# A block's second MLP product: its output gate multiplied into the weights in DRAM, the residual preloaded into accumulators, sums placed at other steps

## The chip, the cores and the metric

The kernel runs on one core of one Trainium2 chip. The metric is the device time of one execution in microseconds (us). TensorE (PE) multiplies matrices into PSUM, VectorE (DVE) and GpSimd (POOL) do elementwise work, ScalarE (ACT) does functions and copies, and SyncE (SP) issues the transfers between DRAM and SBUF, in the order of its queue.

## The reference

One layer of a diffusion block: modulation, three token mixers, an output projection into a gated residual, then a squared-ReLU MLP into a second gated residual, and a final RMS norm. The change touches only the last lines:

```python
x = x + gt1 * (y_lat @ w_out)
x = x + gt2 * (square(relu(modulate(rmsnorm(x, g_mlp), sh2, sc2) @ w_mlp1 + b_mlp1)) @ w_mlp2 + b_mlp2)
return rmsnorm(x, g_final)      # x: 1024 tokens x 1024, w_mlp1: 1024 x 4096, w_mlp2: 4096 x 1024
```

`gt2` (g2 below) is one number for each of the 1024 output columns.

## The kernel before

**Arithmetic.** All large products are done in f32 with two fp32r parts: each operand is split into a high part (a copy by ACT) and a low part (a subtraction by DVE, line 1277), and each product becomes three matmuls. Both MLP products use the seven-product scheme of Winograd for 2 x 2 blocks, so sums and differences of operand blocks are formed first (`qop`, line 1304, on DVE) and sums of results afterwards.

**First product** (`prod1`, `op1`). The 4096 hidden columns are eight f-blocks of 512. Each f-block is seven products, n = 0 to 55 over all; `op1(n + 4)` prepares the operand of a product four ahead and, at an f-block's first product, loads its four quarters of w_mlp1 (line 1301). Each product is 24 matmuls into two PSUM banks. Results go through DVE sums and two ACT passes into one of two staging buffers and from there to DRAM tensor `HD` (line 1365).

**Second product** (`prod2`, `op_ab`, `blk_load`). The 4096 rows of w_mlp2 are taken as f-block 0, then the pairs (1,2), (3,4), (5,6): four blocks `b` of seven products `m` in the order 1, 2, 5, 6, 3, 7, 4. Each product is four PSUM tiles of 128 x 512 (6 matmuls each in block 0, 12 in the others). They are added over the blocks into `PART[1]` to `PART[7]`, four tiles each; in block 0 an ACT copy (line 1563) starts them, in the others DVE adds them (line 1565). `PART[2]` to `PART[5]` are the tiles `acc`, which end as the four quarters of the output. Operands come from a ring `QR` of eleven buffers, among them the two halves of the tile named `rw` and the units `qxh`, `qxl`, `qt`, `uu`.

**Last product.** f-block 7 is multiplied without the scheme: for each of eight token tiles (i, t) and both column halves h, 12 matmuls into one bank, added to the accumulator (line 1623). Its operands are split by `last_op`; those named `lop` (keys b11 and b21) lie in a new tile that takes the place of `rw`. Before this addition the seven sums are folded into the four accumulators (`fold`, line 1524, DVE), each accumulator is multiplied by g2 (line 1536, POOL, 16 instructions), and x2, the first residual with g2 x b_mlp2 already in it, is added from buffers that `x2_load` fills (line 1537, DVE, 16 instructions); two of these buffers are halves of `rw` and a unit `qxl`. Since the accumulators are scaled before f-block 7 comes in, that f-block's weights are multiplied by g2 when they are loaded (line 1460, POOL, 4 loads). Then follow squares for the norm (ACT), the reciprocal root (POOL, line 1629), the scaling (DVE, line 1633) and the store.

**Order.** The program is written in one order; a scheduler ahead of time gives each engine's queue its order from priorities (the written order) and its own estimate of when each instruction is ready. On the chip each queue runs strictly in its order.

Of the kernel before, what the change touches and what calls it, by code (L numbers as in the profile page):

```python
# [7 lines left out]
F32 = mybir.dt.float32  # L8
F32R = mybir.dt.float32r
AF = mybir.ActivationFunctionType  # L10
ALU = mybir.AluOpType
# [4 lines left out]
P = 128  # L16
D = 1024
# [21 lines left out]
def body(nc, tc, a, out):  # L39
    V, S, G, T, SY = nc.vector, nc.scalar, nc.gpsimd, nc.tensor, nc.sync  # L40
# [100 lines left out]
    drp = est.enter_context(pool("drp", space=DRAM))  # L141
# [310 lines left out]
    for d in range(2):  # L452
        r = slice(64 + 32 * d, 96 + 32 * d)
# [275 lines left out]
    with ExitStack() as st:  # L729
# [10 lines left out]
        for hb in range(2):  # L740
            SY.dma_start(out=WRG[64 * hb:64 * hb + 64, :, 64 * hb:64 * hb + 64],
                         in_=a["w_rg"][0].rearrange("d g (t hb) c e -> hb c (d g t) e", hb=2)[hb])
# [425 lines left out]
    X2D = drp.tile([8, P, D], F32, name="X2D")  # L1168
# [4 lines left out]
    g2B = p2a.tile([P, D], F32, name="g2B")  # L1173
    AX1 = p2a.tile([P, 2048], F32, name="ax1")
    AX2 = p2a.tile([P, 1536], F32, name="ax2")
# [88 lines left out]
    w1, w2 = a["w_mlp1"][0], a["w_mlp2"][0]  # L1264
# [5 lines left out]
    def half(ap, n):  # L1270
        return ap.rearrange("p (a n) -> p a n", n=n)
# [34 lines left out]
    def op1(n):  # L1306
        fb, m = n // 7, n % 7
        if fb >= 8:
            return
        q = ORDER1[m]  # L1310
        src = rq[AIN[q]]
        if n < 2:
            src = WRAW
            w1_load(0, AIN[q], src)
        if m == 0:
            for k in ("21", "22", "11", "12"):
                w1_load(fb, k, rq[k])
        if q == 6:
            e = G if n < 7 else V
            qop(rq, "21", "21", "22", ALU.add, e)  # L1320
            qop(rq, "11", "21", "11", ALU.subtract, e)
        elif q == 7:
            qop(rq, "21", "22", "11")
        elif q == 3:
            qop(rq, "12", "12", "11")
        d = R1[(0, 1, 0, 1, 2, 3, 4)[n] if n < 7 else (n - 7) % 6]
        split(src, d[:, 0:1024], d[:, 1024:2048])
        ops1.append(tuple(half(d[:, i:i + 1024], 256) for i in (0, 1024)))
# [95 lines left out]
    prod1(4)  # L1424
    op1(7)
    op1(8)
    for n in range(5, 56):
        prod1(n)
        op1(n + 4)


    ORDER = (1, 2, 5, 6, 3, 7, 4)
# [12 lines left out]
    def cacc(i, h, t):  # L1445
        return PART[2 + 2 * i + h][t]

    def q_load(n, key, fbs, dst):
        r, c = int(key[1]) - 1, int(key[2]) - 1
        if key[0] == "a":  # L1450
            src = HD[fbs[c], r] if len(fbs) == 2 else HD[fbs[0], r, :, 2 * c:2 * c + 2, :]
        else:
            r0, nr = (fbs[r] * 512, 512) if len(fbs) == 2 else (fbs[0] * 512 + r * 256, 256)
            src = w2[r0:r0 + nr, 512 * c:512 * c + 512].rearrange("(s p) c -> p s c", p=P)
        d = half(dst, 512)
        ld[0] = SY.dma_start(out=d, in_=src)
        if key[0] == "b" and fbs == (7,):
            for s_ in range(0, d.shape[1], 2):
                o = d[:, s_:s_ + 2, :]
                G.tensor_tensor(out=o, in0=o, in1=g2B[:, 512 * c:512 * c + 512].unsqueeze(1).broadcast_to([P, 2, 512]), op=ALU.mult)  # L1460

    QS = {}

    def blk_load(b, keys):
        q = QS.setdefault(b, {})
        for k in keys:
            if b == 0:
                u = LOADS.index(k)
                d = XAu[u // 2][:, 1024 * (u % 2):1024 * (u % 2) + 1024]
            else:  # L1470
                d = QR[qn[0] % len(QR)]
                qn[0] += 1
            q[k] = d
            q_load(b, k, BLK[b], d)
# [36 lines left out]
    def blk_t1(b):  # L1511
        if b < len(BLK):
            qop(QS[b], "b12", "b12", "b11")
# [8 lines left out]
    def fold(o, x0, x1, ts=range(4)):  # L1522
        for t in ts:
            V.tensor_tensor(out=PART[o][t], in0=PART[x0][t], in1=PART[x1][t], op=ALU.add)  # L1524

    X2U = {}

    def x2_load():
        for (i, h), k in zip(((0, 0), (0, 1), (1, 1), (1, 0)), ("b11", "b21", "a22", "b12")):
            X2U[i, h] = u = half(QS[NBK - 1][k], 512)  # L1530
            SY.dma_start(out=u, in_=X2D[4 * i:4 * i + 4, :, 512 * h:512 * h + 512].rearrange("t p c -> p t c"))

    def residual(i, h, ts=range(4)):
        for t in ts:
            o = cacc(i, h, t)
            G.tensor_tensor(out=o, in0=o, in1=g2B[:, 512 * h:512 * h + 512], op=ALU.mult)  # L1536
            V.tensor_tensor(out=o, in0=o, in1=X2U[i, h][:, t, :], op=ALU.add)

    LQ, LO = {}, {}

# [14 lines left out]
    def prod2(b, m):  # L1555
        q = ORDER[m]
        oa, ob = OA.pop(0), OB.pop(0)
        for t in range(4):
            ps = pP.get([P, 512])
            mm3(ps, oa, ob, slice(t * P, t * P + P), True, True)  # L1560
            o = PART[q][t]
            if b == 0:
                S.activation(out=o, in_=ps, func=AF.Copy)
            else:
                V.tensor_tensor(out=o, in0=o, in1=ps, op=ALU.add)  # L1565

    blk_load(0, LOADS)
    blk_t1(0)
    op_ab(0, 0)
    op_ab(0, 1)  # L1570
# [2 lines left out]
    for b in range(NBK):  # L1573
        fin = b == NBK - 1
        for m in range(7):
            if m == 0 and not fin:
                with tc.issue_after(ld[0].ins):
                    blk_load(b + 1, LOADS[:3])
            if m == 0 and fin:
                last_load((0, 2, 4))  # L1580
            prod2(b, m)
            if m < 5:
                op_ab(b, m + 2)
            if m == 4 and not fin:
                blk_load(b + 1, LOADS[3:])
                blk_t1(b + 1)
            if m >= 5:
                op_ab(b + 1, m - 5)
            if fin and m == 4:
                last_load((6,))  # L1590
                ow = units(ml.tile([P, 4096], F32R, tag="rw", name="lop"))
                last_op("b11", ow[0])
                last_op("b21", ow[1])
            if fin and m == 5:
                for k, u in zip(("a11", "a12", "b12", "b22"), RAu[e5:e5 + 2] + RBu[e5:e5 + 2]):
                    last_op(k, u)
                rF = QS[b]["a12"][:, 0:1024]
                bcast_row(rF, a["g_final"])
                x2_load()
                fold(7, 7, 6)  # L1600
                fold(5, 5, 7)
                residual(0, 0)
            if fin and m == 6:
                last_op("a21", RAu[2 - e5])
                last_op("a22", RAu[3 - e5])
                residual(0, 1)
            if fin and m == 3:
                fold(6, 6, 1)
                fold(2, 2, 1)
                fold(1, 6, 5)  # L1610
            if fin and m == 4:
                fold(3, 3, 1)
    pP = Sub(PD[0][:2] + pp)
    for i in range(2):
        for t in range(4):
            tc_ = slice(t * P, t * P + P)
            ss = p2a.tile([P, 6], F32, tag="ss3", bufs=4, name="ss3")
            for h in range(2):
                ps = pP.get([P, 512])
                for j in range(2):  # L1620
                    mm3(ps, LO[f"a{i + 1}{j + 1}"], LO[f"b{j + 1}{h + 1}"], tc_, j == 0, j == 1)
                o = cacc(i, h, t)
                V.tensor_tensor(out=o, in0=o, in1=ps, op=ALU.add)
                S.activation(out=psx, in_=o, func=AF.Square, scale=1.0 / 32, accum_out=ss[:, 4 + h:5 + h])
                if i + t == 4:
                    V.tensor_tensor(out=WX[h], in0=o, in1=rF[:, 512 * h:512 * h + 512], op=ALU.mult)
            rs = ss[:, 2:3]
            V.tensor_scalar(out=ss[:, 1:2], in0=ss[:, 4:5], scalar1=ss[:, 5:6], scalar2=EPS, op0=ALU.add, op1=ALU.add)
            G.tensor_tensor(out=rs, in0=ss[:, 1:2], in1=MHALF, op=ALU.pow)
            for h in range(2):  # L1630
                o, dst = cacc(i, h, t), out[0, (4 * i + t) * P:(4 * i + t + 1) * P, 512 * h:512 * h + 512]
                if i + t < 4:
                    V.scalar_tensor_tensor(out=o, in0=o, scalar=rs, in1=rF[:, 512 * h:512 * h + 512], op0=ALU.mult, op1=ALU.mult)
                elif h == 0:
                    S.activation(out=o, in_=WX[h], func=AF.Copy, scale=rs)
                else:
                    V.tensor_scalar(out=o, in0=WX[h], scalar1=rs, scalar2=None, op0=ALU.mult)
                SY.dma_start(out=dst, in_=o)
            if i == 0:
                fold(4, 4, 7, (t,))  # L1640
                residual(1, 0, (t,))
                residual(1, 1, (t,))
    est.close()


# [21 lines left out]
```

## Time and profile before

| | |
|---|---|
| median of three runs | 1337.53 us (1336.25 to 1340.71) |
| the profiled execution, whole | 1332.67 us |
| its span, first to last instruction | 1331.0 us |
| mean granted TensorE clock | 0.979 |
| busy: PE / DVE / ACT / POOL | 93% / 73% / 44% / 20% of the span |
| DMA | 148.64 MB, 33.5% of 16 engines' time |

All rows of the trace have times in us from the span's start. The first product runs in about 703 to 989, the second in 989 to 1259, the last in 1259 to the end. A matmul's end is modelled, so consecutive starts, not durations, give the pace of PE.

### The profile page before, as it was taken

What the parts mean: (1) busy time and instruction counts of PE and PEld (TensorE: products, weight loads), DVE (VectorE), ACT (ScalarE), POOL (GpSimd) and SP (SyncE); (2) the same over time, 40 slices, a digit from 0 to 9 for tenths busy, and PEclk for the clock granted to TensorE, in tenths of its full rate; (3) what the DMA queues carried; (4) which work ended last, traced back from release to release, by engine and by line L of the source; (5) the groups of instructions that cost most, each with busy time, mean ns of one, the idle gap of its engine ahead of it and who ended that gap; (6) DMA issues with size and microseconds to landing.
All of it is one profiled execution on the core that took longest, in us unless ns stands there. A gap on an engine that the chain in (4) does not pass through costs nothing.

```text
span 1331.0 us, 16443 instructions
## 1 busy us (share of the span) xinstructions
PE 1242.2 (93%) x6146; PEld 974.1 (73%) x6146; DVE 972.1 (73%) x1414; ACT 587.7 (44%) x938; POOL 260.3 (20%) x291
## 2 busy tenths in 40 slices
PE   5889998899999899999979999999999999999957
PEld 1567676787786577777857888888888888888746
DVE  4796795888774566775598665555485979899975
ACT  4648653433433434453456444445467333333212
POOL 3321123123220334313650000000000000110541
PEclk9998999999999999999989999999999999999979
DMA  9422233232234221153325322233294050512202
GB/s 326 141 79 84 90 104 95 80 100 92 92 99 119 80 56 56 54 184 136 104 78 174 111 95 95 95 127 127 73 359 153 31 222 1 201 53 80 95 16 111
DMA packets 102483, 148.64 MB, mean 112 GB/s; under 512 B 8870, under 2 KB 62852, under 8 KB 100868
## 3 DMA queue, kind: packets, MB, share of 16 engines
q1 hardware_dynamic: 102404, 147.60, 33.5%
q8 instruction: 48, 0.79, 0.2%
q14 instruction: 31, 0.25, 0.1%
HBM read 116.62 MB, written 30.95 MB: 111 GB/s over the span
## 4 chain that ended last, share of the span: by engine, by line
PE 59%; DVE 10%; POOL 3%; DMA 3%; issue 2%; ACT 2%; POOLq 0%; DVEq 0%; ACTq 0%; SPq 0%
PE pp L53 26%; PE pd L53 19%; PE psx L53 6%; PE psa L53 2%; PE psb L53 2%; POOL acc L1536 1%; PE pst L53 1%; DMA wx<-in_w_out_dram 1%; PE psl L53 1%; PE pst L942 1%; DVE acc L1524 1%; DVE yl L1152 1%; DMA wx<-ZD 1%; DVE rbd L842 1%; DVE yt L1277 1%
## 5 line engine op out<-in xcount | busy, mean ns | idle before, releaser
L53 PE MATMUL pd<-xl,wht 128*128 128x512 f32 (+1 forms) x304 | 124.3, 413 | 5.0 <-DVE xl L235 4.1
L53 PE MATMUL pd<-xh,wlt 128*128 128x512 f32 (+1 forms) x304 | 125.3, 414 | 1.2 <-POOL cp L395 0.7
L53 PE MATMUL pd<-xh,wht 128*128 128x512 f32 (+1 forms) x304 | 124.0, 413 | 1.2 <-ACT cp L647 0.6
L1460 POOL TENSOR_TENSOR qt<-qt,g2B 128x1024 f32<-128x1024 f32 x4 | 11.5, 2902 | 461.1 <-DMA qt<-in_w_mlp_dram 461.1
L352 POOL TENSOR_TENSOR wlt<-wraw,wht 128x512 fp32r<-128x512 f32 x40 | 57.3, 1434 | 177.7 <-ACT wht L351 165.5
L53 PE MATMUL pp<-ya,wlt 128*128 128x512 f32 x188 | 71.8, 391 | 0.0
L53 PEld LDWEIGHTS pd<-xl,wht 128*128 128x128 f32 (+1 forms) x304 | 57.5, 189 | 18.2 <-DVE xl L235 5.7
L53 PE MATMUL pp<-yb,wlt 128*128 128x512 f32 x176 | 68.6, 390 | 0.0
L53 PE MATMUL pp<-ya 128*128 128x512 f32 x176 | 68.5, 389 | 0.0
L53 PEld LDWEIGHTS pd<-xh,wht 128*128 128x128 f32 (+1 forms) x304 | 57.5, 189 | 13.9 <-ACT cp L647 1.0
L53 PEld LDWEIGHTS pd<-xh,wlt 128*128 128x128 f32 (+1 forms) x304 | 57.4, 189 | 14.0 <-issue 1.9
L53 PE MATMUL pd<-ob,yb 128*128 128x512 f32 x220 | 66.8, 396 | 0.0
L727 DVE SCALAR_TENSOR_TENSOR wx<-wx,SCL,wx 128x512 f32<-128x512 f32 x56 | 44.3, 791 | 23.9 <-DMA wx<-in_w_ada_dram 23.6
L351 ACT ACTIVATE wht<-wraw 128x512 fp32r<-128x512 f32 (+2 forms) x50 | 28.6, 580 | 65.8 <-PE pd L53 22.5
L1536 POOL TENSOR_TENSOR acc<-acc,g2B 128x512 f32<-128x512 f32 x16 | 36.8, 2319 | 74.9 <-PE pp L53 52.8
L1304 DVE TENSOR_TENSOR rw<-rw 128x1024 f32<-128x1024 f32 (+1 forms) x31 | 39.9, 1290 | 13.1 <-DMA rw<-in_w_mlp_dram 12.7
L53 PE MATMUL pp<-ob,yb 128*128 128x512 f32 x152 | 46.2, 406 | 2.7 <-DVE acc L1565 2.7
L53 PEld LDWEIGHTS pd<-ob,yb 128*128 128x128 f32 x220 | 41.3, 188 | 9.9
L1276 ACT ACTIVATE ya<-rw 128x1024 fp32r<-128x1024 f32 x26 | 27.4, 1059 | 43.4 <-PE pp L53 22.9
L1362 ACT ACTIVATE pp<-pp,V 128x512 f32<-128x512 f32 x40 | 26.4, 661 | 41.2 <-DVE pp L1357 41.0
L53 PE MATMUL psx<-xc,wht 128*128 128x256 f32 (+1 forms) x192 | 41.7, 297 | 1.2 <-POOL xc L235 0.7
L1357 DVE TENSOR_TENSOR pp<-pp,uu 128x512 f32<-128x512 f32 x40 | 27.8, 696 | 19.6 <-PE pp L53 19.4
(805 smaller groups left out, 3498.6 us busy)
## 6 DMA issues: line engine op xcount, KB each, us to landing
wx<-in_w_ada_dram SPq DMA_DIRECT2D x64, 256.0 KB, 2.8
rw<-in_w_mlp_dram SPq DMA_DIRECT2D x32, 512.0 KB, 4.0
wraw<-in_w_in_dram SPq DMA_DIRECT2D x44, 256.0 KB, 3.1
ada<-in_w_ada_dram SPq DMA_DIRECT2D x16, 512.0 KB, 5.5
HD<-wraw SPq DMA_DIRECT2D x16, 512.0 KB, 3.3
HD<-g1B SPq DMA_DIRECT2D x16, 512.0 KB, 3.0
XB<-XSD SPq DMA_DIRECT2D x19, 256.0 KB, 2.9
xin<-in_x_dram SPq DMA_DIRECT2D x8, 512.0 KB, 5.5
```

Of the source, the lines that this page charges most:

```text
L53: return T.matmul(o, l, r, start=start, stop=stop)
L351: S.activation(out=ph, in_=pr, func=AF.Copy)
L352: (V if split or name[0:2] == "xr" else G).tensor_tensor(out=pl, in0=pr, in1=ph.bitcast(F32), op=ALU.subtract)
L727: V.scalar_tensor_tensor(out=ACCA, in0=t, scalar=SCL[:, k, 0:1], in1=ACCA, op0=ALU.mult, op1=ALU.add)
L842: V.tensor_tensor(out=bd[0:64], in0=row[0:64].unsqueeze(1).broadcast_to([64, nh, P]), in1=IB[0:64, 0:nh].unsqueeze(2).broadcast_to([64, nh ...
L942: T.transpose(pt[:, j, :], t[:, j, :], ident)
L1152: V.tensor_tensor(out=YL[i][:, k, :], in0=ys, in1=YH[i][:, k, :].bitcast(F32), op=ALU.subtract)
L1276: S.activation(out=hi[:, c], in_=src[:, c], func=AF.Copy)
L1304: RS[2] = (e or V).tensor_tensor(out=q[o], in0=q[x0], in1=q[x1], op=op)
L1357: V.tensor_tensor(out=ps, in0=ps, in1=u if q in (2, 4) else w, op=ALU.add)
L1362: S.activation(out=ps, in_=ps, func=AF.Relu, bias=V2[:, 40 + f:41 + f])
L1536: G.tensor_tensor(out=o, in0=o, in1=g2B[:, 512 * h:512 * h + 512], op=ALU.mult)
```

## The change

- A DRAM tensor `W2S` takes w_mlp2 x g2. At n = 12 to 44 of the first product, one row tile after the other (32 tiles of 128 x 1024) is loaded into one of three buffers, multiplied by g2 on POOL and stored; `q_load` reads W2S in place of w_mlp2, and the multiplication at line 1460 goes.
- x2 is loaded into the accumulators of `PART[2]`, `PART[3]` and `PART[4]` ahead of block 0, and block 0's results of these three are added by DVE where ACT copied them. The fourth quarter's x2 goes into the unit of the key a22, and is added in the last product.
- The 16 multiplications at line 1536 and 12 of the 16 additions at line 1537 go. The seven folds stay seven (28 instructions), with other operands and at other steps.

```diff
+    W2S = drp.tile([4096, D], F32, name="W2S")
+    w2b = [AX1[:, 0:1024], AX1[:, 1024:2048], AX2[:, 0:1024]]
+
+    def w2_scale(r):
+        if 0 < r <= 32:
+            SY.dma_start(out=W2S[(r - 1) * P:r * P, :], in_=w2b[(r - 1) % 3])
+        if 0 <= r < 32:
+            u = w2b[r % 3]
+            SY.dma_start(out=u, in_=w2[r * P:(r + 1) * P, :])
+            G.tensor_tensor(out=u, in0=u, in1=g2B, op=ALU.mult)
+
     for n in range(5, 56):
         prod1(n)
         op1(n + 4)
+        with tc.issue_after(ld[0].ins):
+            w2_scale(n - 12)
...
-            src = w2[r0:r0 + nr, 512 * c:512 * c + 512].rearrange("(s p) c -> p s c", p=P)
-        d = half(dst, 512)
-        ld[0] = SY.dma_start(out=d, in_=src)
-        if key[0] == "b" and fbs == (7,):
-            for s_ in range(0, d.shape[1], 2):
-                o = d[:, s_:s_ + 2, :]
-                G.tensor_tensor(out=o, in0=o, in1=g2B[:, 512 * c:512 * c + 512].unsqueeze(1).broadcast_to([P, 2, 512]), op=ALU.mult)
+            src = W2S[r0:r0 + nr, 512 * c:512 * c + 512].rearrange("(s p) c -> p s c", p=P)
+        ld[0] = SY.dma_start(out=half(dst, 512), in_=src)
...
-    X2U = {}
-    def x2_load():
-        for (i, h), k in zip(((0, 0), (0, 1), (1, 1), (1, 0)), ("b11", "b21", "a22", "b12")):
-            X2U[i, h] = u = half(QS[NBK - 1][k], 512)
-            SY.dma_start(out=u, in_=X2D[4 * i:4 * i + 4, :, 512 * h:512 * h + 512].rearrange("t p c -> p t c"))
-    def residual(i, h, ts=range(4)):
-        for t in ts:
-            o = cacc(i, h, t)
-            G.tensor_tensor(out=o, in0=o, in1=g2B[:, 512 * h:512 * h + 512], op=ALU.mult)
-            V.tensor_tensor(out=o, in0=o, in1=X2U[i, h][:, t, :], op=ALU.add)
+    def x2_load(i, h, d):
+        ld[0] = SY.dma_start(out=half(d, 512), in_=X2D[4 * i:4 * i + 4, :, 512 * h:512 * h + 512].rearrange("t p c -> p t c"))
...
-            if b == 0:
+            if b == 0 and q not in (2, 3, 4):
                 S.activation(out=o, in_=ps, func=AF.Copy)
             else:
                 V.tensor_tensor(out=o, in0=o, in1=ps, op=ALU.add)
     blk_load(0, LOADS)
+    with tc.issue_after(ld[0].ins):
+        for i, h in ((0, 0), (0, 1), (1, 0)):
+            x2_load(i, h, acc[2 * i + h])
...
-                x2_load()
-                fold(7, 7, 6)
-                fold(5, 5, 7)
-                residual(0, 0)
+                X2B = QS[b]["a22"]
+                x2_load(1, 1, X2B)
             if fin and m == 6:
                 last_op("a21", RAu[2 - e5])
                 last_op("a22", RAu[3 - e5])
-                residual(0, 1)
-            if fin and m == 3:
+            if fin and m == 0:
                 fold(6, 6, 1)
                 fold(2, 2, 1)
-                fold(1, 6, 5)
-            if fin and m == 4:
-                fold(3, 3, 1)
+            if fin and m == 2:
+                fold(3, 3, 5)
+            if fin and m == 3:
+                fold(3, 3, 6)
+                fold(7, 7, 6)
...
             if i == 0:
                 fold(4, 4, 7, (t,))
-                residual(1, 0, (t,))
-                residual(1, 1, (t,))
+                fold(5, 5, 7, (t,))
+                V.tensor_tensor(out=PART[5][t], in0=PART[5][t], in1=half(X2B, 512)[:, t, :], op=ALU.add)
```

## Rows read from the trace of the kernel before

**Rows 1.** Page, busy us of each engine (share of the span) xinstructions.

```profile
PE 1242.2 (93%) x6146; PEld 974.1 (73%) x6146; DVE 972.1 (73%) x1414; ACT 587.7 (44%) x938; POOL 260.3 (20%) x291
```

**Rows 2.** Windows of the three stages: stretch, us, busy and (instructions), PEclk, DMA share, GB/s.

```profile
702.00:989.00 287.00, 286.53 (x1252) 234.53 (x1251) 180.92 (x202) 142.19 (x195) 0.00 (x0) 1.00 0.39 133
989.00:1259.00 270.00, 270.00 (x1174) 220.08 (x1173) 236.47 (x224) 110.31 (x127) 27.72 (x12) 1.00 0.32 116
1259.00:1331.00 72.00, 48.72 (x192) 37.42 (x190) 48.51 (x73) 14.71 (x36) 24.95 (x16) 0.85 0.16 58
```

**Rows 3.** Waits of PE, 690 to the end: total us, times, longest us.

```profile
PE pd L53 <- ACT lop L1276: 13.7, 1, 13.7
```

**Rows 4.** Timeline of PE, last product: start, us, instructions, [idle before <-releaser].

```profile
1258.78 1.56 PE L53 MATMUL pd<-ob,yb 128*128 128x512 f32 x6
...
1264.13 1.43 PE L53 MATMUL pp<-ob,yb 128*128 128x512 f32 x5 [2.38 <-DVE acc L1565]
1265.92 2.93 PE L53 MATMUL pp<-ob,yb 128*128 128x512 f32 x6 [0.36 <-DVE acc L1565]
...
1285.71 3.33 PE L53 MATMUL pd<-lop,yb 128*128 128x512 f32 x6 [13.74 <-ACT lop L1276]
...
1290.49 1.57 PE L53 MATMUL pp<-lop,yb 128*128 128x512 f32 x6
...
1322.70 1.55 PE L53 MATMUL pd<-ob,ya 128*128 128x512 f32 x6
```

**Rows 5.** Tile views of lop (a wait) and rw (its last users: min/median/max ns).

```profile
  DVE acc L1537: 25.2, 1
...
L1537 DVE TENSOR_TENSOR acc<-acc,rw x4: 679/686/693, 1275.1 to 1283.9; 128x512 f32<-128x512 f32 x4
L1277 DVE TENSOR_TENSOR yb<-rw,ya x3: 1221/1224/1224, 1196.2 to 1219.2; 128x1024 fp32r<-128x1024 f32 x3
```

**Rows 6.** Timeline of POOL at the start of the last product.

```profile
1259.41 15.63 POOL L1536 TENSOR_TENSOR acc<-acc,g2B 128x512 f32<-128x512 f32 x5 [8.24 <-DVE acc L1524]
```

**Rows 7.** Windows of one f-block of the first product, and of its end.

```profile
789.00:827.00 38.00, 38.00 (x167) 31.17 (x167) 21.93 (x26) 18.16 (x25) 0.00 (x0) 1.00 0.33 106
960.00:990.00 30.00, 30.00 (x132) 24.53 (x132) 22.98 (x26) 15.89 (x23) 0.00 (x0) 1.00 0.91 314
```

**Rows 8.** Timelines of POOL and DVE where both work from SBUF.

```profile
1137.52 5.86 POOL L1460 TENSOR_TENSOR qt<-qt,g2B 128x1024 f32<-128x1024 f32 x2 [438.42 <-DMA qt<-in_w_mlp_dram]
...
1138.27 6.19 DVE L1277 TENSOR_TENSOR wht<-qxl,yb 128x1024 fp32r<-128x1024 f32 x2
...
1170.00 2.84 DVE L1277 TENSOR_TENSOR yb<-qt,ya 128x1024 fp32r<-128x1024 f32 x1 [1.54 <-ACT ya L1276]
...
681.14 6.08 POOL L1384 TENSOR_TENSOR xq<-xq,t 128x1024 f32<-128x1024 f32 x2 [4.03 <-DVE t L1375]
...
682.12 2.88 DVE L1377 TENSOR_TENSOR yt<-t,yt 128x512 fp32r<-128x512 f32 x1
```

**Rows 9.** DMA issues, 690 to 993: count, KB each, median us to landing.

```profile
rw<-in_w_mlp_dram SPq DMA_DIRECT2D x28, 512.0 KB, 4.0
```

**Rows 10.** SP: one wait of its queue (690 to 1010), and two issues.

```profile
SPq L1365 <- ACT g1B L1363: 137.7, 16, 16.5
...
960.47 0.32 SPq L1456 DMA_DIRECT2D qxl<-HD  x1
...
979.77 0.34 SPq L1365 DMA_DIRECT2D HD<-g1B  x1
```

**Rows 11.** Block 0: the copies into acc (tile view), DVE's longest idle time (timeline).

```profile
L1563 ACT ACTIVATE acc<-pp x7: 576/579/599, 995.9 to 1027.6; 128x512 f32<-128x512 f32 x7
...
1021.09 2.36 DVE L1277 TENSOR_TENSOR ya<-rw,wlt 128x1024 fp32r<-128x1024 f32 x2 [12.05 <-ACT ya L1276]
```

**Rows 12.** Timeline of DVE: folds, and the scaling of two output tiles.

```profile
1231.80 1.89 DVE L1524 TENSOR_TENSOR acc<-acc,ax 128x512 f32<-128x512 f32 x3
...
1304.99 1.41 DVE L1633 SCALAR_TENSOR_TENSOR acc<-acc,ss,qxh 128x512 f32<-128x512 f32 x2 [0.66 <-POOL ss L1629]
```

## The prediction

> **What bounds the kernel now.** The page's first part makes PE the engine to look at: 93% busy [rows 1]. A share over the whole span hides where the other 7% lies, so the second view is the windows of the three stages that the change touches. PE is busy in 286.5 of 287 us of the first product and in all of the 270 us of the second's four blocks, at full clock; in the last product it is busy in 48.7 of 72 us, at a granted clock of 0.85 [rows 2]. So nothing taken from DVE, ACT or POOL ahead of 1259 can shorten the kernel: there it can only cost. What can be won lies after 1259.
>
> The waits of PE name it: one stall of 13.7 us, for ACT's `lop` [rows 3]. The timeline of PE gives the whole loss. Its last product starts at 1258.78 and ends at 1322.70 + 1.55 = 1324.25, 65.5 us. It has 16 tiles x 12 = 192 matmuls, 32 groups of six. An undisturbed group starts 1.40 us after the one before (16 groups fill the 22.4 us from 1290.49, and six take 1.57 by the model of their ends) [rows 4]. 32 x 1.40 + 0.16 = 45.0 us, so 20.5 us are lost: 13.74 us for `lop`; 2.38 + 0.36 us for DVE's line 1565, which frees PSUM banks late; and the rest mostly as matmuls after each pause at half speed (six in 3.33 and in 2.93 us).
>
> Why is `lop` late? Its tile view says that ACT waited 25.2 us for DVE's line 1537; `rw`'s says that four of the 16 x2 additions read `rw` until 1283.9, while its last operand reader had started by 1219.2 [rows 5]. `lop` takes `rw`'s place. And these additions stand behind POOL's multiplications: five in a row take 15.63 us from 1259.41 [rows 6]. So the chain is fold, POOL multiplication, x2 addition out of `rw`, `lop`, PE.
>
> **The change part by part.**
>
> *The end: 16 multiplications and 12 additions go, x2's last buffer is no longer in `rw`.* `rw` is free after its last operand split, 1219.2 + 1.2 = 1220.4 [rows 5], 38 us ahead of the last product, and the fold-multiply-add chain is gone. What is late next could only be DVE. From the product m = 3 on (four products of 48 matmuls, 44.3 us) it has 16 additions from PSUM and 12 folds at 1.89 / 3 = 0.63 us [rows 12], and 18 splits at 1.22 us [rows 5] (12 for m = 4 to 6, six for the last product): 28 x 0.63 + 18 x 1.22 = 39.6 us of 44.3. It fits. In the last product's first half (22.4 us) it has for each of four token tiles two PSUM additions, two folds and one x2 addition (5 x 0.63) and the scaling (1.41), 4.6 us, and two splits once: 4 x 4.6 + 2.4 = 20.8 us; the second half is lighter by 12 x 0.63 us. Seven PSUM banks hold 7 x 2.8 us of PE's work between. So PE should run through, at full clock since it doesn't pause: 20.5 us gained. The tail after the last matmul (1331.0 - 1324.25 = 6.8 us) stays.
>
> *Folds at other steps.* 28 before, 28 after; eight move from m = 3 to m = 0 and four from m = 4 to m = 2, where PE covers them: 12 x 0.63 = 7.6 us more for DVE ahead of 1220, against what line 1460 no longer costs it (5.5 us, below). I take 0, with 0 to 2 us as bounds.
>
> *g2 into the weights.* 32 loads and 32 stores of 512 KB and 32 multiplications of 128 x 1024 on POOL, during 33 products of the first product; four multiplications go. An f-block there takes 38.2 us (168 matmuls, by 167 in 38.0 [rows 7]), a product 5.5 us. Three resources:
> - POOL: 2.93 us each [rows 8], 20.5 us for an f-block's seven. It has nothing else to do there [rows 2].
> - DMA: seven tiles are 7 x 2 x 0.524 = 7.3 MB in 38.2 us, 192 GB/s. The share per GB/s is 0.91 / 314 at the first product's end and 0.33 / 106 within it [rows 7], so 0.56 to 0.60 more on top of 0.33: 0.89 to 0.93. Tight, but under 1. A load of w_mlp1, 4.0 us now [rows 9], will take longer; its operand is prepared four products (22 us) ahead.
> - DVE, through POOL. Where both worked from SBUF, DVE's two splits took 6.19 us against 2 x 1.22 with two multiplications beside them, 1.9 us lost for each; a split took 2.84, 1.6 us lost; in the stage before, a 128x512 operation took 2.88 against 0.63, 2.2 us lost [rows 8]. DVE's own work is 21.93 us in 38.0 [rows 7]. With 1.6 to 2.2 us for each of seven: 22.0 + 11.2 to 15.4 = 33.2 to 37.4 us of 38.2. It fits at both ends, and PE has seven banks and four prepared operands between. I take 0, by the splits' rows, which are the same operations.
>
> The Trainium skill speaks against this part: its page SBUF — State Buffer (Who interferes with whom) says that GpSimd and a DVE operation with two SBUF inputs take a port as an exclusive lock for the whole instruction, and the loser blocks. The 6.19 us row agrees in kind. By it each multiplication could cost DVE its full length, which is rival A.
>
> *x2 ahead of block 0.* Three loads of 1 MB are 3.1 MB, 9 us of DMA at 345 GB/s, into a stretch with 0.91 of the DMA taken [rows 7]. They stand behind block 0's operands and ahead of most of block 1's in SP's queue. The first result that is added on x2 comes at 995.9, and DVE idles 12.05 us later in block 0 [rows 11], so operands of block 1 that come 6 us late (9 less the free 0.09 of 30 us) are covered; bounds 0 to 6 us, 0 taken. The 12 additions that go from ACT to DVE are 7.6 us of DVE, inside the same idle time.
>
> *Sum.* The profiled span goes from 1331.0 to 1310.5 us. The profiled execution, 1332.67 us, lies 4.9 us under the median of the runs, 1337.5. I take the 20.5 us off the median: **1317.0 us**. With the bounds (0 to 6 us for x2, 0 to 2 us for the folds) and some 3 us of scatter among the runs shown, 1314 to 1324 us.
>
> **The rivals.**
> - **A, the lock costs its full price.** Each multiplication blocks DVE for 2.93 us: 22.0 + 20.5 = 42.5 us in an f-block of 38.2; 4.3 us x 32 / 7 = 20 us are lost and the gain is eaten: 1337 us. For it: the exclusive wait in rows 8. Against: DVE works from SBUF on both inputs in only part of its time there, and idles 42% of it [rows 7]. Chance 0.07, half of it with a part of the loss.
> - **B, another operand or bank is late at the last product.** DVE would be at 39.6 of 44.3 us; a bad order in its queue brings back the smaller stall of now: 2.74 us and 1.5 us of slow matmuls [rows 4], once or twice: 1321 to 1326 us. Chance 0.15.
> - **C, the SP queue becomes the bound, slower than before.** If store r stands ahead of load r + 1, as it is written, a tile takes load 4.0 [rows 9], multiplication 2.93 [rows 8] and two issues of 0.33 [rows 10] one after the other, 7.6 us against 5.5 for a product. SP falls 2.1 x 32 = 67 us behind, and loads of w_mlp1 and stores of HD stand behind; less the 22 us for which operands are ahead, 45 us are lost: 1362 us. It decides from 5.5 us for a tile on. For it: SP does wait in its queue for other engines, 137.7 us for ACT alone [rows 10]. Against: the queue's order is not the written one (a load for the second product was issued at 960.47, a store of the first at 979.77 [rows 10]), and with three buffers a load can go ahead of the store. Chance 0.08. The Trainium skill's DMA: Bandwidth & Descriptors (Anatomy of one DMA) says that a semaphore wait is held by the issuing sequencer before dispatch, which is this mechanism.
> - **D, it doesn't do what it says:** something else than x2 holds `rw`, `lop` stays late, about 1337 us. Rows 5 show no later reader. Chance 0.04.
>
> **How the numbers follow.** The forecast has 0.66. The range holds it and B and a little more on its lower side: 1313 to 1330 us, which leaves out C, D and most of A, 0.2. A measurement of this kernel can tell about 0.3%, 4 us, from no change: faster is under 1333.5. Faster: 0.66 + 0.15 + 0.04 (half of A) = 0.85; same: 0.03 (A) + 0.04 (D) = 0.07; slower: 0.08 (C).
>
> **What would show it.** Right: the timeline of PE has no idle time of a microsecond after 1259 and no matmuls at half speed, `lop` is split before 1250, and the last product takes 45 to 46 us. The first product still takes 287 us for 702 to 989, with a DMA share near 0.9 while the tiles pass. Wrong: waits of PE for DVE or ACT within the first product (A), for line 1301's loads with SP waiting for POOL (C), for DVE's line 1565 at the start of the last product (B), or block 0 starting late for x2.

## The result and the profile after

| | before | after |
|---|---|---|
| median (range), four runs each on one chip | 1337.99 us (1336.25 to 1340.71) | 1318.18 us (1317.43 to 1319.51) |
| ratio after / before, 95% interval | | 0.984 (0.9821 to 0.9858) |
| profiled execution, whole / span | 1332.67 / 1331.0 us | 1317.9 / 1316.2 us |
| busy: PE / DVE / ACT / POOL, share of the span | 93 / 73 / 44 / 20% | 94 / 75 / 44 / 23% |
| DMA moved | 148.64 MB | 182.20 MB |

The change makes the kernel 19.8 us faster by the medians; 20.5 were forecast, and the time is 1.2 us above the forecast.

The windows of the three stages after the change (us; busy us and instructions of PE, PEld, DVE, ACT, POOL; granted clock of PE; DMA share; GB/s) answer to [rows 2]; the last is cut at the end of the span:

```profile
702.00:989.00 287.00, 286.53 (x1245) 234.21 (x1245) 200.95 (x197) 134.17 (x188) 92.99 (x33) 0.99 0.69 242
989.00:1259.00 270.00, 270.00 (x1174) 219.84 (x1173) 243.94 (x246) 111.81 (x125) 0.00 (x0) 1.00 0.35 127
1259.00:1316.00 57.00, 50.48 (x218) 40.35 (x216) 36.90 (x61) 14.31 (x35) 5.15 (x8) 0.97 0.20 74
```

The first line has the price of the stream: POOL 93 us, where it had none, DVE 20 us more, DMA share 0.69 for 0.39. None of it reaches PE in this profile, which stays at 286.53 of 287 us. The gain is in the timeline of PE in the last product (start, us for the group):

```profile
1264.51 1.56 PE L53 MATMUL pd<-lop,yb 128*128 128x512 f32 x6
1265.92 1.56 PE L53 MATMUL pd<-lop,wht 128*128 128x512 f32 x6
1267.32 1.56 PE L53 MATMUL pd<-ob,yb 128*128 128x512 f32 x6
...
1307.92 1.56 PE L53 MATMUL pd<-ob,ya 128*128 128x512 f32 x6
```

From 1264.51 to 1307.92 + 1.56 = 1309.48 are 45.0 us, against 65.5 [rows 4]: a group each 1.40 us, no idle time, and the product now begins with `lop`, the operand that had held it up. The tile view of `lop` says when its high parts (ACT) and low parts (DVE) were made (ns min/median/max, first and last start):

```profile
L1276 ACT ACTIVATE lop<-qt x2: 1042/1054/1067, 1225.7 to 1226.6; 128x1024 fp32r<-128x1024 f32 x2
L1277 DVE TENSOR_TENSOR lop<-qt,lop x2: 1211/1212/1212, 1251.1 to 1252.3; 128x1024 fp32r<-128x1024 f32 x2
```

All are ready 11 us ahead of the product. In [rows 4] PE stood 13.74 us for this tile.

**Why the two profiled spans differ by 14.8 us and not by 20.5.** The chain of work at the first product's start, of after and then of the unchanged kernel profiled once more (e1):

```profile
709.34 4.55 PE pd L53 x20
```

```profile
713.99 4.58 PE pd L53 x20
```

In the profile of before it starts at 703.57, in after's at 709.34, and in e1, which is the kernel before word for word, at 713.99. So this start scatters by 10 us without any change, and a pair of spans can't be subtracted. What can be compared is the stretch from the first product's start to the last's: 1258.78 - 703.57 = 555.2 us before, 1264.51 - 709.34 = 555.2 after. The second measure is the last product: 65.5 and 45.0.

### The profile page after: what moved, and what is told of

The parts are those of the page before. It is cut to its first block, busy times and chain, and to the rows that moved or that the text cites. A ratio compares the mean times of both kernels' runs of the same rounds, so it can differ in the third digit from the quotient of the medians.

```text
span 1316.2 us, 16543 instructions
## 1 busy us (share of the span) xinstructions
PE 1241.0 (94%) x6146; PEld 972.9 (74%) x6146; DVE 981.1 (75%) x1414; ACT 578.2 (44%) x926; POOL 303.8 (23%) x303
## 2 busy tenths in 40 slices
DMA packets 111700, 182.20 MB, mean 138 GB/s; under 512 B 9894, under 2 KB 63876, under 8 KB 110084
## 4 chain that ended last, share of the span: by engine, by line
PE 64%; DVE 7%; POOL 2%; DMA 2%; ACT 1%; issue 1%; POOLq 0%; DVEq 0%; ACTq 0%; SPq 0%
PE pp L53 29%; PE pd L53 19%; PE psx L53 7%; PE psa L53 2%; PE psb L53 2%; PE psl L53 2%; PE pst L53 1%; PE pst L942 1%; DMA wx<-ZD 1%; DMA wx<-in_w_out_dram 1%; DVE rbd L842 1%; POOL xp L993 1%; DVE yt L1277 1%; POOL KV L1035 0%; DVE xp L403 0%
## 5 line engine op out<-in xcount | busy, mean ns | idle before, releaser
L1436 POOL TENSOR_TENSOR ax<-ax,g2B 128x1024 f32<-128x1024 f32 x32 | 90.1, 2833 | 134.7 <-DMA ax<-in_w_mlp_dram 134.7
L1629 POOL TENSOR_TENSOR ss<-ss,V 128x1 f32<-128x1 f32 x8 | 5.1, 643 | 377.2 <-DVE ss L1628 377.2
L1304 DVE TENSOR_TENSOR rw<-rw 128x1024 f32<-128x1024 f32 (+1 forms) x31 | 47.0, 1518 | 33.9 <-DMA rw<-in_w_mlp_dram 33.5
L53 PE MATMUL pp<-ob,yb 128*128 128x512 f32 x152 | 44.5, 395 | 0.0
L53 PEld LDWEIGHTS pp<-ya,wlt 128*128 128x128 f32 x188 | 35.3, 188 | 7.5
```

What stands on the lines that cost most here:

```text
L53: return T.matmul(o, l, r, start=start, stop=stop)
L1304: RS[2] = (e or V).tensor_tensor(out=q[o], in0=q[x0], in1=q[x1], op=op)
L1436: G.tensor_tensor(out=u, in0=u, in1=g2B, op=ALU.mult)
```

## The experiments

Every theory in the expectations goes back to the same question: is the gain the freed `lop`, and is the rest of the change (stream, preload, folds) free, as the sum of the prediction has it? "After" is the changed kernel; ratios are against the kernel before on the same chip.

### The kernel before once more, and after twice more

> The kernel before, profiled a second time. In the profile of the changed kernel the first product starts 5.8 us later than in that of before (709.3 against 703.6), though nothing ahead of it was changed. Theory (scatter among executions): this profile's first product starts somewhere in 703 to 711 as well, and the time is 1336 to 1341 us. Rival (the change delays the early part): it starts at 703.6 again, within 1 us. Both expect the last product to take 65.5 us, with one stall of 13.7 us for lop.

e1 took 1345.35 us with a span of 1343.6, a single execution. Its first product starts 10.4 us later than in the first profile; this and the time lie outside what either theory expected. From there to the last product are again 555.2 us, `lop` holds PE for 12.9 us, and the last product takes 67.7 us, 2.2 more than in the first profile. The scatter of that start lies ahead of everything that the change touches; what makes it was not followed.

> The changed kernel once more, as the measure for the runs beside it: 1317 to 1320 us, last product 44.9 us.

> The changed kernel, as the measure for the two runs beside it: 1317 to 1320 us.

The two repeats gave 1319.78 us (1318.77 to 1323.12), ratio 0.9856 (0.9834 to 0.9877), and on another chip 1319.38 us (1319.2 to 1323.15), ratio 0.9856 (0.9839 to 0.9873). The last product is 45.0 us in both. The stretch ahead of it was 559.8 us in the first and 556.0 in the second, against 555.2: the first product can lose 0 to 4.6 us after all. The profile of the first repeat shows where most of it goes, in the timelines of PE, SP and DVE around 940 us:

```profile
945.47 2.97 PE L53 MATMUL pp<-ob,yb 128*128 128x512 f32 x12
950.51 4.56 PE L53 MATMUL pp<-ob,yb 128*128 128x512 f32 x12 [2.07 <-ACT wraw L1363]
```

```profile
925.52 0.77 SPq L1365 DMA_DIRECT2D HD<-g1B  x1
933.42 0.32 SPq L1432 DMA_DIRECT2D W2S<-ax  x1
933.83 0.39 SPq L1301 DMA_DIRECT2D rw<-in_w_mlp_dram  x1
934.31 0.84 SPq L1365 DMA_DIRECT2D HD<-wraw  x1
935.20 0.50 SPq L1301 DMA_DIRECT2D rw<-in_w_mlp_dram  x1
935.79 1.40 SPq L1365 DMA_DIRECT2D HD<-g1B  x1
937.28 1.33 SPq L1301 DMA_DIRECT2D rw<-in_w_mlp_dram  x2
```

```profile
947.29 1.23 DVE L1304 TENSOR_TENSOR rw<-rw 128x1024 f32<-128x1024 f32 x1 [8.80 <-DMA rw<-in_w_mlp_dram]
948.44 0.69 DVE L1357 TENSOR_TENSOR pp<-pp,uu 128x512 f32<-128x512 f32 x1
```

To be read from SP: nothing goes out for 7 us before the store of `W2S` at 933.42, which waits for the last multiplication (POOL starts it at 930.4). Four loads of w_mlp1 and two stores of `HD` stand behind it. The last load lands at 947.3, and DVE waits 8.80 us for it; the sum that frees a PSUM bank (line 1357) stands behind that on DVE, ACT's result behind the sum, PE behind ACT. PE idles 2.07 us, and its next twelve matmuls take 4.56 us where twelve took 2.97, at a granted clock of 0.63: after the pause part of the stretch runs at the lower level of 1.2 GHz, where all of 940 to 948 had 1.00, 2.4 GHz. This is rival C's place and mechanism at a tenth of its price.

The hold alone does not make the loss. In after's first profile SP sends nothing out for as long before the same store, from 922.57 to 929.68, and PE does not wait (timeline of SP):

```profile
921.78 0.79 SPq L1365 DMA_DIRECT2D HD<-g1B  x1
929.68 0.32 SPq L1432 DMA_DIRECT2D W2S<-ax  x1
```

What differs is how late the store is: counted from the first product's start it goes out at 220.3 us there, at 221.1 us in the second repeat, where PE waits 0.53 us, and at 223.5 us in the first, where it waits 2.07.

### e2: only `lop` freed from the x2 buffer

```diff
-        for (i, h), k in zip(((0, 0), (0, 1), (1, 1), (1, 0)), ("b11", "b21", "a22", "b12")):
+        for (i, h), k in zip(((0, 0), (0, 1), (1, 1), (1, 0)), ("b11", "b21", "a22", "a21")):
```

> The kernel before with one thing changed: the x2 quarter that lay in a half of rw goes into the unit of the key a21, which is free after its split near 1229. All 16 POOL multiplications and 16 x2 additions stay. Theory (lop waits for rw's last reader): lop is split before 1255, the stall of 13.7 us and the slow matmuls behind it (1.8 us) go, gain 15 to 20 us, 1318 to 1323 us. Rival (the POOL multiplications themselves hold the end, through accumulators that are not ready and PSUM banks that are not freed): PE fills its seven banks and then waits for DVE's line 1623; gain under 8 us, 1330 us or more.

One word of the kernel before, and 1325.48 us (1324.29 to 1326.94), ratio 0.9894 (0.9874 to 0.9915): 13.0 us of the 18.7 that the whole change gains on this chip, and short of the 15 to 20 expected. The last product takes 51.4 us for 65.5. What is left, by PE, DVE and POOL:

```profile
1274.83 2.93 PE L53 MATMUL pp<-lop,yb 128*128 128x512 f32 x6 [4.67 <-DVE acc L1565]
```

```profile
1270.49 2.48 DVE L1537 TENSOR_TENSOR acc<-acc,qt 128x512 f32<-128x512 f32 x4
1272.90 2.47 DVE L1565 TENSOR_TENSOR acc<-acc,pp 128x512 f32<-128x512 f32 x4
```

```profile
1268.91 15.94 POOL L1536 TENSOR_TENSOR acc<-acc,g2B 128x512 f32<-128x512 f32 x5 [5.37 <-DVE acc L1524]
```

The four additions that free PSUM (line 1565) come behind four x2 additions and eight folds in DVE's queue; PE waits 4.67 us for them and then runs a group in 2.93 us. This stall was 2.74 us in before [rows 4] and 3.97 in e1. So freeing `lop` is worth 65.5 - 51.4 = 14.1 us of the last product (16.3 from e1's 67.7), and what the rest of the change takes off the end the other 51.4 - 45.0 = 6.4. That the multiplications are what counts there is argued and not shown: e6 below brings the additions back without a loss, but no run takes the multiplications off by themselves.

### e3: no stream at all

```diff
-        with tc.issue_after(ld[0].ins):
-            w2_scale(n - 12)
...
-            src = W2S[r0:r0 + nr, 512 * c:512 * c + 512].rearrange("(s p) c -> p s c", p=P)
+            src = w2[r0:r0 + nr, 512 * c:512 * c + 512].rearrange("(s p) c -> p s c", p=P)
```

The second product reads w_mlp2 itself, so g2 is left out of this result.

> The changed kernel without the stream of w_mlp2 through POOL and DRAM; the second product reads w_mlp2 itself, so the factor g2 is left out of the result. Theory (the stream lies wholly beside PE's work): the time of the changed kernel within 2 us. Rival A (POOL's use of the port costs DVE and so PE) or C (SP's queue): faster than the changed kernel by 4 us or more. DVE's busy time in the first product falls by about 20 us to that of before (181 us) in either case.

1318.70 us (1315.86 to 1319.21), ratio 0.9839 (0.9816 to 0.9863); after on the same chip 1319.78. The stream of 32 loads, 32 multiplications and 32 stores costs 1.1 us by these medians, less than their ranges tell apart. Its single profile has 555.2 us from the first product to the last.

### e4 and e5: the stream made dearer

```diff
             G.tensor_tensor(out=u, in0=u, in1=g2B, op=ALU.mult)
+            u8 = u.rearrange("p (a b) -> p a b", b=P)
+            G.tensor_tensor(out=u8, in0=u8, in1=ones.unsqueeze(1).broadcast_to([P, 8, P]), op=ALU.mult)
```

> The changed kernel with each of the 32 row tiles multiplied twice on POOL (the second time by ones). POOL's work in an f-block of the first product goes from 7 x 2.83 = 19.8 us to 39.6 us of 38.2. Theory (a multiplication costs DVE 0.8 us, as the profile of the changed kernel shows, and DVE is not the bound): DVE has 24 + 5.6 = 30 us of 38.2 in an f-block, PE loses little, 0 to 10 us, through tiles that come late and hold SP's queue: 1318 to 1329 us. Rival A (each multiplication blocks DVE for its full length): 22 + 39.6 = 62 us of DVE in an f-block of 38.2, 1400 us or more.

1385.78 us (1384.86 to 1389.98), ratio 1.0346 (1.0318 to 1.0374): both theories missed, one below and one above. The second factor is ones. DVE is not full: it is busy 30.3 of 38, 18.6 of 38 and 19.8 of 39 us in three successive stretches from 778. The timelines of SP, ACT and PE around 820 us show what does:

```profile
811.76 6.03 SPq L1432 DMA_DIRECT2D W2S<-ax  x2
817.85 0.42 SPq L1435 DMA_DIRECT2D ax<-in_w_mlp_dram  x1
822.20 0.32 SPq L1432 DMA_DIRECT2D W2S<-ax  x1
822.56 0.43 SPq L1365 DMA_DIRECT2D HD<-g1B  x1
823.09 0.74 SPq L1301 DMA_DIRECT2D rw<-in_w_mlp_dram  x1
```

```profile
826.88 0.60 ACT L1363 ACTIVATE g1B<-pd 128x512 f32<-128x512 f32 x1 [10.39 <-DMA HD<-g1B]
827.37 1.05 ACT L1276 ACTIVATE wlt<-rw 128x1024 fp32r<-128x1024 f32 x1
```

```profile
827.53 4.75 PE L53 MATMUL pd<-yt,yb 128*128 128x512 f32 x12 [9.32 <-ACT g1B L1363]
```

Three stores of `W2S`, each held for its multiplication, keep the store of `HD` back until 822.56; ACT needs the staging buffer of that store and stands 10.39 us; PE needs the bank that ACT empties and stands 9.32 us. ACT had four such waits, 41.5 us together. PE's waits in the first product end on this pass of ACT for 40.1 us, and for 10.5 us on DVE's sums (line 1353), whose own cause was not followed. So the second multiplication hurt mostly through SP.

```diff
-            SY.dma_start(out=W2S[(r - 1) * P:r * P, :], in_=w2b[(r - 1) % 3])
+            SY.dma_start(out=W2S[(r - 1) * P:r * P, :], in_=w2b[0])
...
-            u = w2b[r % 3]
+            u = w2b[0]
```

> The changed kernel with one buffer for the row tiles in place of three, so that load, multiplication and store of successive tiles can't overlap: about 5.3 + 2.8 + 2.6 us and two waits, 11 us for a tile, against 5.5 us for a product. Rival C (SP's queue decides once a tile takes longer than a product): the queue falls up to 32 x 5.5 = 176 us behind, loads of w_mlp1 and stores of HD wait behind it, and PE loses tens of us: 1350 us or more. If SP's order lets the other transfers pass, or the tiles simply end later (there are 60 us between the last tile and the first product's end), the loss is under 10 us.

1365.83 us (1363.85 to 1369.04), ratio 1.019 (1.0167 to 1.0213). With one buffer, load, multiplication and store follow one another: the tiles come every (1045.2 - 738.1) / 31 = 9.9 us, against (926.3 - 740.4) / 31 = 6.0 in after. The multiplications of e5 (tile view) and what SP waited for:

```profile
L1436 POOL TENSOR_TENSOR ax<-ax,g2B x32: 2337/2402/3373, 738.1 to 1045.2; 128x1024 f32<-128x1024 f32 x32
```

```profile
SPq L1432 <- POOL ax L1436: 194.2, 32, 7.2
...
SPq L1435 <- DMA W2S<-ax: 57.1, 30, 2.3
```

So rival C's mechanism exists, and its end lies on the slow side as forecast. Its arithmetic doesn't hold: e4's tiles take (988.6 - 740.0) / 31 = 8.0 us and cost more than e5's of 9.9. What stands in the queue behind a held store decides, not the time per tile alone. Nor does all of e5's loss lie where rival C puts it, in the first product: its last multiplication starts at 1045.2 us, when the second product has begun. Of some 33 us that PE waits after the first product's start, 22.2 come after 1000: 8.8 us for an operand of the second product whose loads stand behind tiles in SP's queue, 6.9 us for an ACT copy into `ax`, the stream's own buffer, and 6.5 us in four waits for ACT's last pass (line 1363).

### e6 and e7: preload and folds undone

e6 lets ACT start all sums of block 0 again, loads three quarters of x2 into units that come free at the end, and adds them there:

```diff
-            if b == 0 and q not in (2, 3, 4):
+            if b == 0:
...
-        for i, h in ((0, 0), (0, 1), (1, 0)):
-            x2_load(i, h, acc[2 * i + h])
...
+                X2U = {(0, 0): QS[b]["b11"], (0, 1): QS[b]["b21"], (1, 0): QS[b]["a21"]}
+                for i_, h_ in X2U:
+                    x2_load(i_, h_, X2U[i_, h_])
+                x2_add(0, 0)
...
```

> The changed kernel with x2 not preloaded: block 0's results are copied by ACT as before, and three quarters of x2 are loaded into units outside rw and added by DVE at the end (8 additions before the last product, 4 in it). Theory (only rw and the POOL multiplications mattered, DVE has some room): DVE has 42.9 + 8 x 0.63 = 48 us of work in the 44.5 us ahead of the last product, so it comes 3 to 4 us late, which seven PSUM banks hold; 0 to 3 us slower than the changed kernel. Rival (the preload is what frees the end): 8 us or more slower.

e7 makes 12 folds at m = 3, four at m = 4 and four at m = 5:

```diff
-            if fin and m == 0:
+            if fin and m == 3:
...
-            if fin and m == 2:
                 fold(3, 3, 5)
-            if fin and m == 3:
+            if fin and m == 4:
                 fold(3, 3, 6)
+            if fin and m == 5:
                 fold(7, 7, 6)
```

> The changed kernel with the folds at steps like those of the kernel before: twelve at m = 3, four at m = 4, four at m = 5, none at m = 0 and 2. Theory (PE covers the folds wherever DVE has room): within 2 us of the changed kernel. Rival (spreading the sums is needed): the operands of the last product come late and PE stalls; 4 us or more slower.

1319.52 us (1316.9 to 1322.65), ratio 0.9843 (0.982 to 0.9867), and 1321.53 us (1319.28 to 1322.75), ratio 0.9855 (0.9836 to 0.9875): neither can be told from after (0.984 to 0.9856). In both the last product takes 45.0 us. Preloading x2 and spreading the folds gain nothing by themselves; undoing both at once was not run. In e7 DVE has almost no room left ahead of the last product (in e6 none, 49.00 of 49 us), and it still suffices:

```profile
1220.00:1269.00 49.00, 49.00 (x215) 39.95 (x214) 48.05 (x59) 18.68 (x20) 0.00 (x0) 1.00 0.16 55
```

### e8 and e9: the multiplication put elsewhere

```diff
-            SY.dma_start(out=W2S[(r - 1) * P:r * P, :], in_=w2b[(r - 1) % 3])
+            G.dma_start(out=W2S[(r - 1) * P:r * P, :], in_=w2b[(r - 1) % 3])
```

> The changed kernel with the stores of W2S issued from POOL's queue, behind the multiplication, in place of SP's. SP then no longer waits for POOL (120 us in the profile of the changed kernel). Theory (what the stream costs, 0 to 4.6 us in an execution, is transfers of w_mlp1 and HD held behind those waits): loads of w_mlp1 land sooner, PE has no wait within the first product, and the time is 0 to 3 us under the changed kernel's. Rival (the cost is DMA bandwidth, 0.75 of it taken): no change. If issuing costs POOL and DVE more than it saves, slower.

The stores leave SP's queue for POOL's: 1325.50 us (1319.12 to 1328.56), ratio 0.989 (0.9869 to 0.9911), 6 us more than after on the same chip, where the theory expected 0 to 3 us less and the rival no change; it is the third case named, that issuing from POOL costs more than it saves. SP no longer waits for POOL, but now for the stores' ends, and DVE's operand sums (line 1304, 757 to 948) take 2474 ns, against 1489 in after and 1224 in before:

```profile
SPq L1435 <- DMA W2S<-ax: 76.8, 17, 8.4
```

```profile
L1304 DVE TENSOR_TENSOR rw<-rw 128x1024 f32<-128x1024 f32 x18 | 44.5, 2474 | 24.1 <-DMA rw<-in_w_mlp_dram 13.7 <-issue 10.1
```

Its profile, of an execution of 1323.31 us, has 557.8 us from first to last product, 1.8 us over after's on that chip; where the other microseconds of the median go isn't settled. PE still waits within the first product, 1.7 us for DVE's line 1353. So e8 does not confirm that the 0 to 4.6 us come from held transfers: that rests on the rows of the repeats.

e9 drops the stream and multiplies each weight unit by g2 after its load in the second product, as the kernel before does for f-block 7 alone:

```diff
-            src = W2S[r0:r0 + nr, 512 * c:512 * c + 512].rearrange("(s p) c -> p s c", p=P)
-        ld[0] = SY.dma_start(out=half(dst, 512), in_=src)
+            src = w2[r0:r0 + nr, 512 * c:512 * c + 512].rearrange("(s p) c -> p s c", p=P)
+        d = half(dst, 512)
+        ld[0] = SY.dma_start(out=d, in_=src)
+        if key[0] == "b":
+            for s_ in range(0, d.shape[1], 2):
+                o = d[:, s_:s_ + 2, :]
+                G.tensor_tensor(out=o, in0=o, in1=g2B[:, 512 * c:512 * c + 512].unsqueeze(1).broadcast_to([P, 2, 512]), op=ALU.mult)
```

> The changed kernel without the stream: each unit of w_mlp2 is multiplied by g2 on POOL after it is loaded for the second product, as the kernel before did for the last f-block alone. Same 32 multiplications and no extra DMA, but beside the second product, where DVE is busy 244 of 270 us. With 0.8 to 1.9 us of DVE lost for each: 26 to 61 us more, over its 26 us of room. Theory (the place of the multiplications matters through DVE): PE waits for operands, 3 to 35 us slower than the changed kernel. Rival (they hide here as well): within 2 us.

1345.20 us (1342.41 to 1345.61), ratio 1.0035 (1.0022 to 1.0047): slower than before, although its last product takes 45.0 us too. The stretch from the first product to the last grows to 583 us (555.2 to 559.8 in after's three profiles). Two windows of it, and one place in the timelines of POOL and DVE:

```profile
1030.00:1110.00 80.00, 71.57 (x296) 57.13 (x295) 76.86 (x60) 23.43 (x25) 29.11 (x10) 0.94 0.23 82
1110.00:1190.00 80.00, 72.94 (x307) 58.21 (x306) 77.22 (x64) 27.34 (x28) 20.86 (x8) 0.98 0.30 102
```

```profile
1035.79 6.65 POOL L1471 TENSOR_TENSOR qxl<-qxl,g2B 128x1024 f32<-128x1024 f32 x2
```

```profile
1034.13 6.11 DVE L1277 TENSOR_TENSOR ya<-rw,wlt 128x1024 fp32r<-128x1024 f32 x2
```

DVE is busy 96% of these windows; two splits beside two multiplications take 6.11 us, close to the 6.19 of [rows 8]. Of 19.3 us that PE waits after the first product's start, 18.5 end on DVE. In the second product this lands on the busiest engine but PE; in the first product DVE has room. The place of the multiplications is what the detour through DRAM buys.

## Why the prediction came out, step by step

**The bound and the loss at the end: right.** PE runs without a gap through the last product, 45.0 us as worked out from the undisturbed groups [rows 4], and 20.5 us of it are gone. One of its marks failed to the letter: `lop`'s split was to start before 1250 and starts at 1251.1; on the clock of the profile before, 5.8 us earlier by the first product's start, that is 1245.3.

**The chain that was blamed: right, and the smaller part has its size now.** Freeing `lop` alone returns 14.1 us (e2) and the rest of the change 6.4; the prediction had 13.74 for the stall and laid the rest to line 1565 and to slow matmuls, and both are what e2 has left.

**DVE near the end: the room was right, a term was missing.** From 1220 to 1264.5 it is busy 42.9 of 44.5 us where 39.6 of 44.3 were forecast: the sum left out two operand sums of 128x2048 at 2.28 us, 4.6 us, and its other terms came out 1.3 us shorter. It was nearer to rival B than it seemed. In the first half of the last product 18.6 of 22.5 us were measured and 20.8 forecast. e7 with 48.05 of 49 us busy shows that even this would have held.

**The lock between DVE and POOL: taken at 0, and the price behind it was about twice too large.** The forecast lost 1.6 to 2.2 us of DVE for each multiplication and let an f-block reach 33.2 to 37.4 us of 38.2. Five f-blocks of after:

```profile
757.00:795.00 38.00, 38.00 (x167) 31.15 (x167) 26.69 (x25) 17.79 (x25) 17.99 (x7) 1.00 0.74 263
795.00:833.00 38.00, 38.00 (x168) 31.15 (x166) 24.82 (x24) 14.46 (x21) 15.52 (x6) 1.00 0.84 290
...
910.00:948.00 38.00, 38.00 (x168) 31.17 (x167) 23.38 (x25) 17.48 (x25) 11.84 (x4) 1.00 0.60 212
```

DVE is busy 23.4 to 26.7 us. Its groups in 757 to 948 (busy us, mean ns), of which these are the largest:

```profile
L1304 DVE TENSOR_TENSOR rw<-rw 128x1024 f32<-128x1024 f32 x19 | 28.3, 1489 | 33.3 <-DMA rw<-in_w_mlp_dram 33.0
L1277 DVE TENSOR_TENSOR yb<-rw,yb 128x1024 fp32r<-128x1024 f32 x11 | 20.8, 1892 | 6.3 <-ACT yb L1276 6.3
L1277 DVE TENSOR_TENSOR ya<-rw,ya 128x1024 fp32r<-128x1024 f32 x10 | 19.6, 1958 | 10.8 <-ACT ya L1276 10.8
```

With the splits of wht and wlt (9.3 and 8.9 us) they are 51 operations in 86.9 us; undisturbed ones of 1.22 us would take 62.2. That is 24.7 us for the 28 multiplications of this stretch, 0.9 us each (the expectations of e4 and e9 have 0.8). The rows taken for the price [rows 8] are places where a multiplication met DVE's work in full; mostly DVE is waiting or works from PSUM meanwhile. How one collision works can be read from POOL and DVE at 820 us:

```profile
819.55 3.03 POOL L1436 TENSOR_TENSOR ax<-ax,g2B 128x1024 f32<-128x1024 f32 x1 [0.31 <-DMA ax<-in_w_mlp_dram]
```

```profile
820.25 3.42 DVE L1277 TENSOR_TENSOR ya<-rw,ya 128x1024 fp32r<-128x1024 f32 x1
```

POOL ends at 822.58, DVE at 823.67, 1.09 us later: DVE's 1.2 us begin when POOL is done. So here the one that came first went on to its end. The page SBUF — State Buffer (Who interferes with whom) of the Trainium skill says that the port is held as an exclusive lock, and these rows agree. The 0.9 us is an average over multiplications that met DVE's work and others that did not. Rival A needed every multiplication to meet DVE in full.

**DMA: the share was forecast too high.** 0.89 to 0.93 against 0.60 to 0.84 in the five windows; the stream spreads over more time than 33 products (a tile each 6.0 us, not 5.5), and the share per GB/s is 0.0028 to 0.0029, where 0.0029 to 0.0031 were used.

**The stream's cost in time: right in the median, wrong as a plain 0.** By medians it is 1.1 us (e3), in single profiles up to 4.6, by the rows of the first repeat through SP's queue. The prediction put rival C's threshold at 5.5 us for a tile; after runs at 6.0, beyond it, and loses next to nothing. By the prediction's own arithmetic the delay of 0.5 x 32 = 16 us stays within the 22 us for which operands are ahead; that this is the reason was not tested. e4 and e5 show that the fall beyond is steep, 46 to 66 us. The page DMA: Bandwidth & Descriptors (Anatomy of one DMA) of the Trainium skill puts a semaphore wait on the issuing sequencer, ahead of dispatch. SP's rows agree: nothing behind the held store goes out for 7.1 us in the repeat, and for up to 8.1 us in e4.

**Preload and folds: right at 0,** by e6 and e7. The loads of x2 took 11.3 us to land, where 1 MB loads at that place took 6.8 to 11.8 in before, and PE did not wait for one.

**The base: right.** The gain was taken off the median and not off the profiled span, and the medians differ by 19.8 us where the profiles differ by 14.8.

## What to carry to other kernels

Before work is made cheaper, look for the buffer that it shares with a later operand: here one word in a list of buffer names gave 13 of 19 us. Work moved beside a bound engine was free here only while its whole chain kept pace in every queue that it entered; the queue to check first is the in-order one that issues the transfers, since a store that waits there held back loads and stores that have nothing to do with it. And compare stages from mark to mark: spans of single profiles scattered here by more than half of the gain.

## What was not expected of the hardware

- Doubling POOL's work beside DVE did not fill DVE (18.6 to 30.3 us of 38): it cost 66 us, mostly through SP's queue.
- Stores issued from POOL's queue went with DVE operations on two SBUF inputs of 2474 ns where they took 1489 with SP's stores; which step of such a store does that, the runs don't show.
- With the stream beside them, unchanged stores of 512 KB from the second staging buffer took 6.5 us to land (3.0 before), those from the first 3.5 (3.3). With the stream's stores in POOL's queue (e8), at the same DMA share of 0.69, they took 3.0 and 3.4: the share alone does not make it.
